# A streaming encoder trunk in fp32r: the last channel tile's gate and store issued earlier, the second half's layer norm written between matmul products, eight tiles for the feed-forward squares

## The chip, the cores and the metric

The kernel runs on one core of one Trainium2 chip. The time is the device time of one launch in microseconds, the median of three runs: 1488.08 us (1486.97 to 1489.66). The engines are TensorE (PE, matrix products), VectorE (DVE), ScalarE (ACT), GpSimd (POOL) and SyncE (SP), which issues most of the loads and stores. Each engine works through its own instructions in the order in which they stand in its program, and waits on semaphores for the others.

## The reference

A trunk of two layers for 512 prompt frames and 8 x 16 sample frames, 640 columns in all, with 1024 channels:

```python
def conv_module(h, hist, g, w_pw1, b_pw1, w_dw, b_dw, ln_g, ln_b, w_pw2, b_pw2):
    a, gate = jnp.split(rms_norm(h, g) @ w_pw1 + b_pw1, 2, axis=-1)
    glu = a * jax.nn.sigmoid(gate)
    full = jnp.concatenate([hist.astype(glu.dtype), glu], axis=1)
    y = lax.conv_general_dilated(full, w_dw[:, None, :], window_strides=(1,), padding="VALID", ...) + b_dw
    y = jax.nn.silu(layer_norm(y, ln_g, ln_b))          # depthwise, width 31; mean and variance per frame
    return h + y @ w_pw2 + b_pw2, full[:, -CONV_HIST:]

def swiglu_ffn(h, g, w_in, w_out):
    a, b = jnp.split(rms_norm(h, g) @ w_in, 2, axis=-1)
    return h + (jax.nn.silu(a) * b) @ w_out

# layer 0: h = conv_module(h); h = swiglu_ffn(h)
# layer 1: h = h + attention(rms_norm(h), shared k, v) @ w_o; h = swiglu_ffn(h); at the end rms_norm(h)
```

The outputs are the normed frames, the keys and values, and the last 30 columns of `glu` of every stream.

## The kernel before

Channels lie on the partitions: `h` has eight channel tiles of 128 partitions by 640 columns. The columns are worked in two halves of 320 (index `g`, 0 or 1; half 0 holds the 128 sample columns and 192 prompt columns, half 1 the other prompt columns). A float32 product is made of three fp32r products: a weight tile `raw` is split into `whi` (rounded, by ACT) and `wlo` (the rest, by DVE), an operand into `xh` and `xl` the same way, and `mm3` (L179 to L185) adds hi x hi, lo x hi and hi x lo. `wsplit` (L133) loads a weight tile and splits it; there are two buffers of each kind. The feed-forwards combine quarter blocks in the manner of Strassen, seven products in place of eight; `X11`, `X21`, `XT4`, `X22` are operands of them, and `XH` and `XL` are their two parts.

**The convolution.** For every channel tile c, `glu_` (L713) makes the two products of the pointwise layer, the tanh (ACT, L726) and the gate (DVE, L733 for the sample columns, L739 for the prompt columns), which writes `gall`. Tiles 0 to 2 are convolved tap by tap on DVE (`conv_taps`, L764 to L779) and POOL. Tiles 3 to 7 are convolved on PE: `conv_shift` (L805) stores the gated tile to a buffer in device memory (`sa` for half 0, `sb` for half 1), `conv_read` (L811) reads it back four times, each shifted by one column (`xa`, `xb`), and `conv_pe` (L818, matmuls at L832) multiplies the copies. The string `PLAN` sets the order in which this is written: `E7` is the gate of tile 7's half 0 with its store and reads, `F7` that of half 1, `S7 A7` its convolution for half 0, `e` the taps of tile 2 on DVE, `n` the layer norm of half 0, `m` that of half 1, `w0 w1` the second pointwise layer of each half.

**The layer norm.** `conv_ln` (L838) goes in four steps, separated by `yield`: the mean (sums on DVE, L212, then matmuls with a column of 1/1024, L221), its spread over the partitions (matmuls with the identity, L233), the subtraction, squares on ACT and their sums (L867); the variance's mean; its spread; the scaling, silu and split into the operands `z`. `staged_ln` (L896) writes the steps of half 0 between the convolutions of tiles 5, 6 and 7 for half 1. `pw2` (L906) makes the second pointwise layer: four weight tiles, each for two channel tiles of the output, 48 matmuls of 320 columns each, 192 for a half; DVE adds the result to `h` (L924).

**The feed-forward's norm.** `stats` (L556) squares the eight tiles of `h`, adds them up, and spreads the reciprocal root over the partitions; the squares pass through two buffers in turn. `xnorm` multiplies it into the operands. `std` (L430) makes the plain products. `MEAN_AT`, `SPREAD_AT` and `STATS1_AT` are the places among earlier products at which the matmuls of the norms stand.

**What sets the order.** The program is written in the order of the source and then put in order engine by engine by a scheduler that goes by its own estimate of the times. The source steers it: `tc.high_priority` lets work go ahead, `tc.issue_after(x)` and `behind(...)` keep work behind an instruction x that is written earlier. On SP and in the engines' queues nothing overtakes afterwards.

Of the kernel before, what the change touches and what calls it, by code (L numbers as in the profile page):

```python
# [15 lines left out]
P = 128  # L16
D = 1024
# [19 lines left out]
MEAN_AT, SPREAD_AT, STATS1_AT = 3, 5, 2  # L37
# [7 lines left out]
GAPS = 1, 12, 2  # L45
# [36 lines left out]
def tile_trunk(ctx, tc, xT, vecs, hist, w_pw1, w_pw2, w_in0, w_out0, w_os0, w_in1, w_out1, w_os1,  # L82
# [50 lines left out]
    def wsplit(src, k, n, parts=1, pool=0, cuts=1, gains=None):  # L133
# [18 lines left out]
        with tc.high_priority(offset=HP):  # L152
            for i in range(cuts):
                a, b = sz * i // cuts, sz * (i + 1) // cuts
                nc.scalar.activation(out=hi[:, a:b], in_=raw[:, a:b], func=AF.Copy)
                c = b - (b - a) * pool // 4
                for eng, a, b in ((nc.vector, a, c), (nc.gpsimd, c, b)):
                    if a < b:
                        eng.tensor_tensor(out=lo[:, a:b], in0=raw[:, a:b],  # L159
                                          in1=hi[:, a:b].bitcast(F32), op=ALU.subtract)  # L160
        return hi, lo
# [68 lines left out]

    def spread(st, r, n, ins=False):
        for t, a in enumerate(tiles(n)):
            end = nc.tensor.matmul(st[:, a:a + P], r[:, t:t + 1].to_broadcast([P, P]), ident,  # L233
                                   start=True, stop=True)
        return end.ins if ins else st[:, :n]
# [68 lines left out]
    def ffn(l, w_in, w_out, w_os, tail, hf, lead=(), b0=None):  # L304
# [280 lines left out]
        with tc.high_priority(offset=HP):  # L585
# [4 lines left out]
            with tc.issue_after(put_end[0]):  # L590
                xnorm(x21, 0, 4)
# [114 lines left out]
    glu_end, gate_end, conv_end, sum_end = [None], [None], [None], [None]  # L706
# [57 lines left out]
    def conv_taps(chains, limit):  # L764
        for i in range(W):
            for c, part, dst, js in chains:
# [10 lines left out]
                else:  # L777
                    nc.vector.scalar_tensor_tensor(out=dst, in0=src, scalar=wj, in1=dst,
                                                   op0=ALU.mult, op1=ALU.add)  # L779
# [25 lines left out]
    def conv_shift(c, tag, c0, n, late=False):  # L805
        nt = NXA if tag == "a" else NXB
        sc = dr.tile([P, nt], F32, tag="s" + tag, name=nm("s" + tag), bufs=3)[:, 0:n]
        nc.sync.dma_start(sc, gall[:, c, c0:c0 + n])
        return (lambda: conv_read(sc, tag, n, nt)) if late else conv_read(sc, tag, n, nt)

    def conv_read(sc, tag, n, nt):  # L811
        x4 = cp.tile([P, 4, nt], F32, tag="x" + tag, name=nm("x" + tag), bufs=2)
        for s in range(4):
            nc.sync.dma_start(x4[32 * s:32 * s + 32, :, 0:n - s],
                              sc[:, s:n].rearrange("(q p) w -> p q w", q=4))
# [90 lines left out]
    def pw2(g, z):  # L906
        n = gr[g][1]
        for m2 in M2[g]:
            if (KT, m2) not in pws:
                pws[KT, m2] = wsplit(w_pw2[m2], 16, P, pool=PL2[g])  # L910
# [5 lines left out]
            for ks in [range(k, k + 1) for k in range(KT)] if both else [range(KT)]:  # L916
                for i in range(2):
                    mm3(pair[i], [(wh[:, (i * 8 + k) * P:(i * 8 + k + 1) * P],
                                   wl[:, (i * 8 + k) * P:(i * 8 + k + 1) * P]) for k in ks],
                        xk(z, ks), ks[0] == 0, ks[-1] == KT - 1)  # L920
# [8 lines left out]
    def step(op, arg):  # L929
# [17 lines left out]
        elif op in "CDEF":  # L947
            if op != "F":
# [8 lines left out]
                nc.sync.dma_start(convs_out[:, c], gs[:, c])  # L957
            if op != "E":
                glu(c, 1, *pws[c])
                if op != "D":  # L960
                    x4s[c][2] = conv_shift(c, "b", NSC + HA, NXB, c == KT - 1)
# [553 lines left out]
```

## Time and profile before

| | us |
|---|---|
| median of three runs | 1488.08 |
| profiled run | 1485.55 |
| its span | 1483.6 |
| PE busy | 1429.4 (96%) |
| DVE busy | 1138.3 (77%) |
| ACT busy | 757.2 (51%) |
| POOL busy | 297.7 (20%) |
| DMA | 192.56 MB, 130 GB/s on average |

The profile shows one execution. Its times count from the span's start. A row of a timeline gives the start, the time that the group of equal instructions took, the engine, the line, the operation, output<-inputs, the number of instructions and, in square brackets, how long the engine had been idle before it and what ended that. `SPq` is SP's queue of DMA issues: the time there is that of the issue, not of the transfer. Matmuls overlap, so the distance of their starts, not the duration of one, is the pace.

### The profile page before, as it was taken

Reading aid. Unit: us, or ns where it says so; the run is one execution under the profiler, and the core shown is the slowest. Engines: PE = TensorE matmul, PEld = TensorE weight load, DVE = VectorE, ACT = ScalarE, POOL = GpSimd, SP = SyncE. Lnnn points to the kernel's source line nnn. Section 1 sums busy time; section 2 is a strip of 40 time slices with the busy share of each in tenths; the row PEclk is TensorE's granted clock in tenths of the full one; section 3 lists DMA queues with packets and bytes.
Section 4 is the critical chain, followed back from the end, with each engine's and each line's share of the span. In section 5 each row is a group of like instructions: output and inputs, shape, how many; then the busy total and the mean of one; then the engine's idle time right before and its main releaser. Section 6 shows DMA issues by size and latency. Waiting matters only on the chain.

```text
span 1483.6 us, 28030 instructions
## 1 busy us (share of the span) xinstructions
PE 1429.4 (96%) x10932; PEld 1365.9 (92%) x10932; DVE 1138.3 (77%) x2523; ACT 757.2 (51%) x1620; POOL 297.7 (20%) x356
## 2 busy tenths in 40 slices
PE   5999899999999999999999999999999999999997
PEld 5998699999999999999988888987899999999997
DVE  5789656799888888866766767566799888888755
ACT  3666245465454564445655454443565455455443
POOL 5789102001111111103222112010001111111101
PEclk9999999999999999999999999999999999999999
DMA  7256514125445444433655555361224444544512
GB/s 239 68 160 189 138 58 136 36 75 143 131 116 133 134 118 130 132 109 133 212 164 204 180 173 193 129 208 23 86 75 129 138 118 117 150 118 108 153 64 72
DMA packets 66660, 192.56 MB, mean 130 GB/s; under 512 B 12000, under 2 KB 30176, under 8 KB 58080
## 3 DMA queue, kind: packets, MB, share of 16 engines
q1 hardware_dynamic: 52736, 161.10, 33.5%
q0 software_dynamic: 13504, 29.37, 9.7%
q8 instruction: 86, 1.41, 0.4%
q14 instruction: 46, 0.38, 0.1%
q10 hardware_dynamic: 288, 0.31, 0.1%
HBM read 179.14 MB, written 11.61 MB: 129 GB/s over the span
## 4 chain that ended last, share of the span: by engine, by line
PE 77%; DVE 8%; POOL 6%; ACT 3%; DMA 3%; issue 3%; SPq 0%; POOLq 0%; DVEq 0%; ACTq 0%
PE mm L409 46%; PE mm L182 8%; PE mm L183 7%; PE mm L184 7%; POOL ca L788 5%; PE am L1226 1%; PE am L1209 1%; PE w L221 1%; PE w L1242 1%; ACT whi L147 1%; PE am L1273 1%; DVE wlo L343 1%; PE mm L832 1%; DVE B L446 1%; PE w L1185 1%
## 5 line engine op out<-in xcount | busy, mean ns | idle before, releaser
L409 PE MATMUL mm<-XH,wlo 128*128 128x320 f32 x896 | 276.9, 310 | 0.0
L409 PE MATMUL mm<-XH,whi 128*128 128x320 f32 x896 | 276.1, 311 | 0.7 <-ACT t L419 0.5
L409 PE MATMUL mm<-XL,whi 128*128 128x320 f32 x896 | 274.4, 310 | 0.0
L342 ACT ACTIVATE whi<-raw 128x512 fp32r<-128x512 f32 (+2 forms) x280 | 169.2, 614 | 141.3 <-PE mm L409 116.5
L182 PE MATMUL mm<-xh,whi 128*128 128x320 f32 (+2 forms) x640 | 202.5, 318 | 6.4 <-ACT xh L171 4.2
L343 DVE TENSOR_TENSOR wlo<-raw,whi 128x512 fp32r<-128x512 f32 (+2 forms) x280 | 184.9, 668 | 22.4 <-ACT whi L342 21.0
L183 PE MATMUL mm<-xh,wlo 128*128 128x320 f32 (+2 forms) x640 | 201.1, 315 | 0.6 <-DVE wlo L159 0.6
L184 PE MATMUL mm<-xl,whi 128*128 128x320 f32 (+2 forms) x640 | 198.4, 313 | 0.0
L409 PE MATMUL mm<-hid,whi 128*128 128x320 f32 x732 | 171.4, 310 | 2.2 <-DVE hid L343 2.2
L409 PEld LDWEIGHTS mm<-XH,whi 128*128 128x128 f32 x896 | 168.4, 189 | 2.1 <-ACT t L419 1.3
L409 PEld LDWEIGHTS mm<-XH,wlo 128*128 128x128 f32 x896 | 169.0, 189 | 0.0
L409 PEld LDWEIGHTS mm<-XL,whi 128*128 128x128 f32 x896 | 167.9, 188 | 0.0
L182 PEld LDWEIGHTS mm<-xh,whi 128*128 128x128 f32 x640 | 122.5, 192 | 9.7 <-ACT xh L171 5.0
L409 PEld LDWEIGHTS mm<-hid,whi 128*128 128x128 f32 x732 | 124.8, 188 | 4.2 <-DVE hid L343 3.2
L183 PEld LDWEIGHTS mm<-xh,wlo 128*128 128x128 f32 x640 | 122.9, 192 | 1.0 <-DVE wlo L159 0.8
L184 PEld LDWEIGHTS mm<-xl,whi 128*128 128x128 f32 x640 | 121.8, 191 | 0.4 <-issue 0.2
L409 PE MATMUL mm<-hid,wlo 128*128 128x320 f32 x366 | 112.9, 308 | 0.0
L409 PE MATMUL mm<-XL,shi 128*128 128x320 f32 x344 | 105.5, 308 | 5.0 <-DVE XL L343 5.0
L409 PE MATMUL mm<-XH,shi 128*128 128x320 f32 x344 | 105.8, 308 | 0.7 <-ACT XH L342 0.7
L409 PE MATMUL mm<-XH,slo 128*128 128x320 f32 x344 | 105.7, 307 | 0.0
L388 POOL DMA_DIRECT2D s<-in_w_in x38 | 22.1, 581 | 386.2 <-DVE wlo L343 207.9
L788 POOL TENSOR_TENSOR ca<-ca,cvt 128x512 f32<-128x512 f32 x60 | 91.7, 1528 | 15.0 <-ACT cvt L785 8.0
(255 smaller groups left out, 3345.2 us busy)
## 6 DMA issues: line engine op xcount, KB each, us to landing
raw<-in_w_in SPq DMA_DIRECT2D x38, 1024.0 KB
s<-in_w_in POOLq DMA_DIRECT2D x76, 256.0 KB, 4.2
raw<-in_w_os SPq DMA_DIRECT2D x24, 768.0 KB
cache<-in_ck SPq DMA_DIRECT2D x32, 512.0 KB
cache<-in_cv SPq DMA_DIRECT2D x32, 512.0 KB
raw<-in_w_pw SPq DMA_DIRECT2D x12, 1024.0 KB
s<-in_w_os POOLq DMA_DIRECT2D x48, 192.0 KB, 3.6
raw<-in_w_kq SPq DMA_DIRECT2D x8, 1024.0 KB
```

The source lines that it names most:

```text
L147: nc.scalar.activation(out=hi[:, a:b], in_=raw[:, a:b], func=AF.Copy, scale=gain)
L182: nc.tensor.matmul(ps, wh, xh, start=(first and i == 0), stop=False)
L183: nc.tensor.matmul(ps, wl, xh, start=False, stop=False)
L184: end = nc.tensor.matmul(ps, wh, xl, start=False, stop=(stop and i == last))
L221: mean_end[0] = nc.tensor.matmul(st[:, 512 + t * w + k:513 + t * w + k], s[:, a:a + P], onec, start=True, stop=True).ins
L342: put_end[1] = nc.scalar.activation(out=hi, in_=src, func=AF.Copy).ins
L343: put_end[0] = nc.vector.tensor_tensor(out=lo, in0=src, in1=hi.bitcast(F32), op=sub).ins
L388: nc.gpsimd.dma_start(s1, src[:, 2 * n:3 * n])
L409: last = nc.tensor.matmul(pt, wt, v, start=(first and k == i == 0), stop=(k == n - 1 and i == 2), skip_group_check=True)
L446: nc.vector.scalar_tensor_tensor(out=out, in0=x, scalar=-1.0, in1=y, op0=mult, op1=op)
L788: nc.gpsimd.tensor_tensor(out=acc, in0=acc, in1=pr, op=ALU.add)
L832: conv_end[0] = nc.tensor.matmul(pt[32 * q:32 * q + 32, 0:n], w4[0:r, 4 * tg + q, :], mv, start=(tg == 0), stop=(tg == 7)).ins
```

## The change

Two stretches of the program get another order, the end of the convolution up to the head of the first feed-forward and the end of the attention up to the head of the second. The number of instructions on each engine stays the same.

1. The first half of tile 7: its store and reads are written ahead of tile 6's half-1 reads and of the output store; the weight loads `w_pw2[0]` and `w_pw2[1]` are issued around tile 6, that of `w_pw2[0]` without its split, and the loads of `w_pw2[2]` and `[3]` stand behind tile 7's half-1 reads.
2. On DVE the taps of tile 2 are parted: 24 behind tile 7's first gate, 13 behind its second gate (token `f`), where the split of `w_pw2[0]` stands too. In the sums of the first mean tiles 2 and 3 change places.
3. The second half's layer norm is written between the products of `pw2(0)`, in gaps of 5, 3, 10 and 4 pieces of six matmuls (`GAPS1`), and the rest behind it. Counted in matmuls of `pw2` on PE: the mean stands behind 30 where it stood behind none (its last third behind 21), its spread behind 48 (43), the variance's mean 60 behind that spread (118), the variance's spread 24 behind its mean (27), and 60 matmuls of this half follow it (4).
4. The feed-forward's norms are placed by 4, 6, 1 (`MEAN_AT`, `SPREAD_AT`, `STATS1_AT`) instead of 3, 5, 2. In the first feed-forward the second half's mean stands behind 74 products (86), its spread 40 behind that (45), and 30 products lie between the spread and the first product with `XT4` (13). In the second they are 97 (98), 23 (40) and 24 (6); there a tie in `std` keeps the second pair of products of the third weight behind the spread.
5. `stats` has a tile of its own for each of the eight squares.

On SP, before, from the store of tile 6's half 1 (`sb`) to the store of tile 7's half 0 (`sa`); `raw` is a weight load, `xb` the shifted reads of tile 6, `out_convs` an output store:

```order
L808 DMA sb_1566<-gall 128x350
L144 DMA raw_2403<-in_w_pw 128x2048
L814 DMA xb_1568<-sb_1566 32x4x350
L814 DMA xb_1568<-sb_1566 32x4x349
L814 DMA xb_1568<-sb_1566 32x4x348
L814 DMA xb_1568<-sb_1566 32x4x347
L957 DMA out_convs<-gall 128x368
L808 DMA sa_1672<-gall 128x590
```

And now, from the same store on; `xa` are the shifted reads of tile 7:

```order
L815 DMA sb_1571<-gall 128x350
L815 DMA sa_1666<-gall 128x590
L983 DMA out_convs<-gall 128x368
L821 DMA xa_1668<-sa_1666 32x4x590
L821 DMA xa_1668<-sa_1666 32x4x589
L821 DMA xa_1668<-sa_1666 32x4x588
L821 DMA xa_1668<-sa_1666 32x4x587
L821 DMA xb_1673<-sb_1571 32x4x350
```

The store moved past a weight load, four reads and an output store, and tile 7's reads past those of tile 6.

On DVE, before, around the gate of tile 7's half 1 (L739); `w_174` is the chain of taps of tile 2, `w_113` another such chain, `acc` the sums of the first mean:

```order
L778 SCALAR_TENSOR_TENSOR w_113_789<-gall,dwv,w_113_789 128x128
L778 SCALAR_TENSOR_TENSOR w_174_1225<-gall,dwv,w_174_1225 128x128 x13
L739 SCALAR_TENSOR_TENSOR gall<-t_226_1836,t_227_1838 128x320
L159 TENSOR_TENSOR wlo_2347<-raw_2345,whi_2346 128x2048
L212 TENSOR_TENSOR acc_1986<-y_102 128x320
L212 TENSOR_TENSOR acc_1986<-acc_1986,y_102 128x320 x5
```

And now, at the same place:

```order
L785 SCALAR_TENSOR_TENSOR w_174_1225<-gall,dwv,w_174_1225 128x128 x5
L746 SCALAR_TENSOR_TENSOR gall<-t_229_1827,t_230_1829 128x320
L785 SCALAR_TENSOR_TENSOR w_174_1225<-gall,dwv,w_174_1225 128x128 x4
L160 TENSOR_TENSOR wlo_1434<-raw_1432,whi_1433 128x2048
L785 SCALAR_TENSOR_TENSOR w_174_1225<-gall,dwv,w_174_1225 128x128 x9
L215 TENSOR_TENSOR acc_1992<-y_102 128x320
L215 TENSOR_TENSOR acc_1992<-acc_1992,y_102 128x320 x5
```

Thirteen taps moved from ahead of this gate to behind it, in two groups around the split. Ahead of tile 7's first gate, the gate of tile 6's half 1 moved in and five taps moved out; the split of 2048 columns stands ahead of it in both.

On DVE in the second half's norm, before, from the subtraction of the mean on (`acc` are the sums of the squares `sql`, `h` the additions of the products):

```order
L851 TENSOR_TENSOR y_103<-y_103,w_255_2191 128x320 x8
L924 SCALAR_TENSOR_TENSOR h<-mm_2293,vec,h 128x320
L924 SCALAR_TENSOR_TENSOR h<-mm_2294,vec,h 128x320
L159 TENSOR_TENSOR wlo_2405<-raw_2403,whi_2404 128x2048
L867 TENSOR_TENSOR acc_2227<-sql_2223 128x320
L924 SCALAR_TENSOR_TENSOR h<-mm_2351,vec,h 128x320
L867 TENSOR_TENSOR acc_2227<-acc_2227,sql_2223 128x320
```

And now:

```order
L943 SCALAR_TENSOR_TENSOR h<-mm_2197,vec,h 128x320
L943 SCALAR_TENSOR_TENSOR h<-mm_2198,vec,h 128x320
L858 TENSOR_TENSOR y_103<-y_103,w_260_2229 128x320 x8
L160 TENSOR_TENSOR wlo_2353<-raw_2351,whi_2352 128x2048
L874 TENSOR_TENSOR acc_2283<-sql_2279 128x320
L943 SCALAR_TENSOR_TENSOR h<-mm_2299,vec,h 128x320
L874 TENSOR_TENSOR acc_2283<-acc_2283,sql_2279 128x320
```

The two additions to `h` moved ahead of the subtractions; both splits of weights still stand ahead of the last sums.

The diff, cut to what bears on this:

```diff
-MEAN_AT, SPREAD_AT, STATS1_AT = 3, 5, 2
+MEAN_AT, SPREAD_AT, STATS1_AT = 4, 6, 1
-GAPS = 1, 12, 2
+GAPS, GAPS1 = (1, 12, 2), (5, 3, 10, 4)
-LNO = ((0, 1, 4, 5, 6, 2, 3, 7), (0, 1, 4, 2, 3, 5, 6, 7))
-PLAN = ("a0 y x1 b0 b1 q0 dp1s0 c2 k ds1p2 D3 C4 S3 q3 ds2 C5 E6 S4 A4 F6 B4 E7 e S5 A5 F7 k k k S6 A6 "
-        "S7 A7 n s0 m w0 w1")
-HELD = {(1, 0): 21, (2, 0): 9}
+LNO = ((0, 1, 4, 5, 6, 3, 2, 7), (0, 1, 4, 2, 3, 5, 6, 7))
+PLAN = ("a0 y x1 b0 b1 q0 dp1s0 c2 k ds1p2 D3 C4 S3 q3 ds2 C5 E6 S4 A4 F6 B4 E7 e S5 A5 F7 f k k k S6 A6 "
+        "S7 A7 n s0 m w1")
+HELD, HELD2 = {(1, 0): 21, (2, 0): 4}, {(2, 0): 14}
...
-        def std(ws, half, sink):
+        def std(ws, half, sink, second=None):
             pa, pb = mmt()[:, :NH], mmt()[:, :NH]
             for k, x in enumerate(((X11, X21), (XT4, X22))[half]):
-                xproduct(pa, ws[k], x, k == 0)
-                ends.append(xproduct(pb, ws[2 + k], x, k == 0).ins)
+                with tc.issue_after(second) if k and second else nullcontext():
+                    xproduct(pa, ws[k], x, k == 0)
+                    ends.append(xproduct(pb, ws[2 + k], x, k == 0).ins)
...
-                            (nc.gpsimd, nc.vector)[half], half == 1)
+                            (nc.gpsimd, nc.vector)[half], half == 1, sqs=x12 + x22)
...
-            with tc.issue_after(put_end[0]):
+            with nullcontext() if b0 is None else tc.issue_after(put_end[0]):
                 xnorm(x21, 0, 4)
...
-            std(wstd[jj], 0, sinks[jj])
+            std(wstd[jj], 0, sinks[jj], jj == 2 and b0 is not None and norm_spread[0])
...
-            with tc.issue_after(conv_end[0]):
+            with behind(conv_end[0], tap_end[0]):
                 next(ln, None)
...
-                pws[KT, m2] = wsplit(w_pw2[m2], 16, P, pool=PL2[g])
+                with tc.issue_after(read_end[0]):
+                    pws[KT, m2] = wsplit(w_pw2[m2], 16, P, pool=PL2[g])
...
+            if both:
+                for k in range(KT):
+                    part(0, range(k, k + 1))
+                    part(1, range(k, k + 1))
+                    yield
+            else:
                 for i in range(2):
...
+                    for k in range(0, KT, 2):
+                        part(i, range(k, k + 2))
+                        yield
...
-                else:
-                    pws[KT, 0] = wsplit(w_pw2[0], 16, P)
                 glu_(c, 0, *pws[c], None)
-                x4s[c] = [w4, conv_shift(c, "a", 0, NSC if op == "D" else NXA), None]
-                nc.sync.dma_start(convs_out[:, c], gs[:, c])
+                read = conv_shift(c, "a", 0, NSC if op == "D" else NXA, True)
+                if c + 2 == KT:
+                    pws[KT, 0] = wsplit(w_pw2[0], 16, P, late=True)
+                    with tc.issue_after(store_end[0]):
+                        pws[KT, 1] = wsplit(w_pw2[1], 16, P)
+                x4s[c] = [w4, read(), None]
+                if c + 1 == KT:
+                    with tc.issue_after(read_end[0]):
+                        x4s[c - 1][2] = x4s[c - 1][2]()
+                with tc.issue_after(store_end[0]):
+                    nc.sync.dma_start(convs_out[:, c], gs[:, c])
...
         elif op == "e":
             with tc.issue_after(gate_end[0]):
-                conv_taps(held, {})
+                conv_taps(held, HELD2)
...
+        elif op == "f":
+            with behind(gate_end[0], glu_end[0]):
+                conv_taps(held, {})
+                pws[KT, 0] = pws[KT, 0]()
...
         elif op == "m":
-            for _ in conv_ln(1, sum_end[0]):
+            ln, products = conv_ln(1, sum_end[0]), pw2(0, zs[0])
+            for gap in GAPS1:
+                for _ in range(gap):
+                    with tc.issue_after(conv_end[0]):
+                        next(products)
+                with tc.issue_after(conv_end[0]):
+                    next(ln, None)
+            while next(products, 0) is None:
                 pass
         elif op == "w":
-            pw2(c, zs[c])
+            for _ in pw2(c, zs[c]):
+                pass
```

More of the change, by code (lines that the diff above doesn't have):

```diff
@@ L151, in wsplit, with split @@
             return hi, lo
[L152 to L161, printed above, removed]
+        def split():
+            with tc.high_priority(offset=HP):
+                for i in range(cuts):
+                    a, b = sz * i // cuts, sz * (i + 1) // cuts
+                    nc.scalar.activation(out=hi[:, a:b], in_=raw[:, a:b], func=AF.Copy)
+                    c = b - (b - a) * pool // 4
+                    for eng, a, b in ((nc.vector, a, c), (nc.gpsimd, c, b)):
+                        if a < b:
+                            eng.tensor_tensor(out=lo[:, a:b], in0=raw[:, a:b],
+                                              in1=hi[:, a:b].bitcast(F32), op=ALU.subtract)
+            return hi, lo
+        return split if late else split()
     @contextmanager
@@ L234, in spread @@
                                    start=True, stop=True)
+        norm_spread[0] = end.ins
         return end.ins if ins else st[:, :n]
@@ L704, in w4t @@
         return cp.tile([P, 1024], F32, tag="w4", name=nm("w4"), bufs=3)
-    glu_end, gate_end, conv_end, sum_end = [None], [None], [None], [None]
+    glu_end, gate_end, conv_end, sum_end, store_end, read_end, tap_end = ([None] for _ in range(7))
     def glu(c, g, wh, wl, mid=None):
```

24 lines of the change are left out of this document (13 added, 11 removed).

## The prediction

> **What bounds the kernel.** The page's table of busy time comes first:
>
> ```profile
> PE 1429.4 (96%) x10932; PEld 1365.9 (92%) x10932; DVE 1138.3 (77%) x2523; ACT 757.2 (51%) x1620; POOL 297.7 (20%) x356
> ```
>
> TensorE (PE) is busy for 96% of the span of 1483.6 us, so only PE's idle time, 54.2 us in all, and stretches at a low clock can be won back by a change of order. The next view is PE's waits between 130 and 300 us, where the conv module ends and the first feed-forward begins; a row gives the total, the count and the longest wait:
>
> ```profile
> PE mm L832 <- DMA xa<-sa: 6.1, 1, 6.1
> PE mm L409 <- DVE XL L343: 2.9, 2, 2.2
> ```
>
> The largest, 6.1 us, is a single wait for a DMA, the shifted copies of the last channel tile. The third view is the chain of waits, read forward to that wait (start, length, what):
>
> ```profile
> 147.46 3.96 DVE w L778 x16
> 151.42 4.56 DMA sa<-gall
> ...
> 159.09 6.50 DMA xa<-sa
> ...
> 165.72 6.77 PE mm L832 x128
> ```
>
> From the start of the store to the arrival of the copies is 159.09 + 6.50 − 151.42 = 14.2 us. The fourth view, busy times by stretch, gives the granted clock (PEclk, the column after POOL) around the waits:
>
> ```profile
> 164.00:170.00 6.00, 4.28 (x76) 4.08 (x80) 0.00 (x0) 0.37 (x1) 0.00 (x0) 0.50 0.72 174
> ...
> 194.00:198.00 4.00, 4.00 (x21) 4.00 (x19) 1.79 (x4) 2.29 (x6) 0.00 (x0) 0.57 0.00 0
> ...
> 226.00:228.00 2.00, 0.92 (x6) 0.88 (x6) 2.00 (x6) 2.00 (x5) 0.00 (x0) 1.00 0.00 0
> 228.00:232.00 4.00, 3.48 (x15) 3.26 (x14) 2.78 (x7) 4.00 (x10) 0.00 (x0) 0.57 0.00 0
> ...
> 290.00:293.00 3.00, 3.00 (x13) 3.00 (x13) 3.00 (x8) 0.48 (x2) 0.00 (x0) 0.50 0.00 0
> ```
>
> After a wait PE runs for a while at half clock. A stretch of 4 us at 0.57 loses 4 × 0.43 = 1.7 us; I use that as the price of one such stretch.
>
> **The last tile's first half.** The timelines of PE, ScalarE (ACT), VectorE (DVE) and SyncE (SP) show why the store starts so late:
>
> ```profile
> 153.75 0.31 PE L183 MATMUL mm<-xh,wlo 128*128 128x320 f32 x1
> ...
> 154.78 0.31 PE L184 MATMUL mm<-xl,whi 128*128 128x320 f32 x1
> 155.02 4.57 PE L832 MATMUL mm<-xa,w 128*32 128x128 f32 x128
> 165.72 6.77 PE L832 MATMUL mm<-xa,w 128*32 128x128 f32 x128 [6.13 <-DMA xa<-sa]
> 172.43 0.83 PE L221 MATMUL w<-onec,acc 128*128 128x1 f32 x6
> ```
>
> ```profile
> 144.12 0.52 ACT L726 ACTIVATE t<-mm,hb 128x320 f32<-128x320 f32 x1
> 155.19 0.53 ACT L726 ACTIVATE t<-mm,hb 128x320 f32<-128x320 f32 x1 [3.05 <-PE mm L184]
> ```
>
> ```profile
> 142.26 2.28 DVE L159 TENSOR_TENSOR wlo<-raw,whi 128x2048 fp32r<-128x2048 f32 x1
> 144.46 1.92 DVE L778 SCALAR_TENSOR_TENSOR w<-gall,dwv,w 128x128 f32<-128x128 f32 x5
> 146.29 0.91 DVE L733 SCALAR_TENSOR_TENSOR gall<-t,t 128x128 f32<-128x128 f32 x1
> 147.12 0.35 DVE L739 SCALAR_TENSOR_TENSOR gall<-t,t 128x192 f32<-128x192 f32 x1
> 147.38 9.96 DVE L778 SCALAR_TENSOR_TENSOR w<-gall,dwv,w 128x128 f32<-128x128 f32 x32
> 157.25 0.49 DVE L739 SCALAR_TENSOR_TENSOR gall<-t,t 128x320 f32<-128x320 f32 x1
> 157.65 2.29 DVE L159 TENSOR_TENSOR wlo<-raw,whi 128x2048 fp32r<-128x2048 f32 x1
> 159.85 0.48 DVE L212 TENSOR_TENSOR acc<-y 128x320 f32<-128x320 f32 x1
> 160.37 2.67 DVE L212 TENSOR_TENSOR acc<-acc,y 128x320 f32<-128x320 f32 x5
> ```
>
> ```profile
> 148.29 1.74 SPq L814 DMA_DIRECT2D xb<-sb  x4
> 150.14 1.19 SPq L957 DMA_DIRECT2D out_convs<-gall  x1
> ```
>
> The gate was ready at 147.47; the store stood on SP behind four reads and an output store until 151.42. In the new order nothing but the earlier tile's store stands ahead of it there. On DVE five taps (1.92) leave the place ahead of the gate, and a 0.49 gate of the sixth tile's second half comes in: with the split ending at 144.5 and the tanh at 144.64, the gate is ready near 146.1 and the store follows at once. With the 14.2 us of before as the upper bound (a load of weights and the reads of xb, which shared the DMA engines then, are elsewhere now) the copies arrive by 160.3. PE needs them at 159.59, the end of the row at 155.02. So the wait of 6.13 falls to between 0 and 0.7, and the 128 matmuls take 4.57 again, not 6.77: PE is through at 164.2 to 164.9, where it was at 172.4.
>
> What is late next is DVE. Thirteen taps of tile 2 now stand behind the gate of the last tile's second half, whose tanh ends at 155.72. One chain of dependent taps costs 1.92/5 = 0.38 each, so: gate 0.41, taps 13 × 0.37 = 4.8, split 2.2, six sums 3.1, end near 166.2. (The other 24 taps cost 24 × 9.96/32 = 7.5 and end by 153.6, before that tanh: hidden.) The mean at 172.43 therefore begins near 166.2, after a PE wait of 1.3 to 2.0. **Gain 6.2.** Whether such a wait brings a half-clock stretch is open, 0 or 1.7; I take off the middle, 0.8. The moved reads of xb feed matmuls that stand behind that mean, and the output store has no reader: both cost nothing unless the reads, now behind those of xa, land after it.
>
> **The second half's layer norm.** These rows price it:
>
> ```profile
> 202.34 3.27 DVE L851 TENSOR_TENSOR y<-y,w 128x320 f32<-128x320 f32 x8 [3.62 <-PE w L233]
> ...
> 215.14 1.01 DVE L867 TENSOR_TENSOR acc<-acc,sql 128x320 f32<-128x320 f32 x2
> ```
>
> ```profile
> 227.08 0.41 PE L182 MATMUL mm<-xh,whi 128*128 128x320 f32 x1 [1.58 <-ACT xh L171]
> 228.74 0.64 PE L182 MATMUL mm<-xh,whi 128*128 128x320 f32 x1 [0.52 <-DVE h L924]
> ```
>
> Before, four products followed the last spread, and PE then waited 1.58 + 0.52 for the normed tiles, with the half-clock stretch at 228 behind it: 3.8 us. Now the rest of the 192 products of the first half, 60 of them, stand behind that spread; at a pace of (154.78 − 153.75)/7 = 0.147 they cover 8.8 us, so these 3.8 go. But the variance's mean now follows the first spread after 60 products (8.8 us), where it had 118. In DVE's order stand between that spread and the last sum: eight subtractions (3.2), two splits (2 × 2.2 to 2.3), and four additions to h and seven sums, of the same 320 columns, at 0.41 (3.27/8) to 0.50 (1.01/2) each, 4.5 to 5.5. That is 12.1 to 13.3, less the two additions that can start while the spread still runs (up to 0.8). PE waits 2.5 to 4.5; I take 3.3, nearer the lower end because the operations overlap at their ends in the trace, and a half-clock stretch behind it, 1.7, as after the 2.1 us at 227. The block of means that precedes the stretch at 194 keeps its size, so that stretch stays. **Net loss 5.0 − 3.8 = 1.2**; ends 1.3 gained (wait 2.5, no stretch) and 2.4 lost (wait 4.5).
>
> **The feed-forward heads.** The rows with waits and the spreads ahead of them:
>
> ```profile
> 282.37 0.83 PE L233 MATMUL w<-ident,rst 128*128 128x128 f32 x6
> 288.76 0.41 PE L409 MATMUL mm<-XL,shi 128*128 128x320 f32 x1 [2.19 <-DVE XL L343]
> ...
> 1066.43 0.83 PE L233 MATMUL w<-ident,rst 128*128 128x128 f32 x6
> 1068.88 0.41 PE L409 MATMUL mm<-XH,shi 128*128 128x320 f32 x1 [0.73 <-ACT XH L342]
> 1073.22 0.41 PE L409 MATMUL mm<-XL,shi 128*128 128x320 f32 x1 [2.04 <-DVE XL L343]
> ```
>
> In the first feed-forward the second half's operand was ready 5.56 us after the spread (283.20 to 288.76), of which PE worked 3.37. Seventeen more products now stand in that gap: 3.37 + 17 × 0.147 = 5.87, enough by 0.3. The wait of 2.19 and the stretch at 290 (1.7) go: **gain 3.9**, ends 2.5 and 3.9. In the second feed-forward eighteen more stand there, 2.6 us against waits of 0.73 + 2.04 = 2.77: **gain 2.3**, between 0, if the waits only move on, and 2.6; I give 0.3 back, since DVE works without a pause there. The sums of squares must be ready twelve products, 1.8 us, sooner; eight tiles in place of two let ACT square without waiting for the adder to release one. These squares lie beside 74 products (10.9 us) and cost PE nothing; if that cover failed, each of them would add one operation of 320 columns, 0.5 at most.
>
> **Sum.** 6.2 − 0.8 − 1.2 + 3.9 + 2.3 = 10.4 us. The profiled run took 1485.55 us, 2.5 less than the median of 1488.08; 1485.55 − 10.4 = 1475.1 there, and 1477.7 as a median.
>
> By the Trainium skill ("TensorE: Matmul & The Clock Gate", Part 1, the clock gate) the array drops to half rate after at least one idle window of about 3.4 us. The stretches here agree with that length, but waits of 2.1 and 2.19 us were enough to bring one, so in this kernel partly idle windows count, and I charge the stretch.
>
> **The rivals.** (a) Part of the tile-7 gain comes back: the store meets other traffic or the sums on DVE end later, and the clock drops at both new waits. Half of 6.2, another 0.9 for the clock: about 1481.7; 16%. For it: DVE has no idle time between 155.7 and 166 in my schedule.
> (b) DVE is the bound in both feed-forward heads and the earlier spread only moves the waits: 6.2 returns, 1483.9; 12%. For it: the margin of 0.3; against it: the waits end on operands whose whole chain starts at the spread.
> (c) The clock does not drop at the new waits of 2.0 and 3.3: 2.5 less, 1475.2; 12%. This is also what the rule of the Trainium skill's page on the clock gate would give.
> (d) Slower. The loads of the last two pointwise weights now stand on SP behind this row:
>
> ```profile
> 179.43 1.74 SPq L814 DMA_DIRECT2D xb<-sb  x4
> ```
>
> With the 6 us gained they go out near 175; a tile of 128 x 2048 numbers of four bytes, 1.05 MB, at 174 GB/s (the rate of the stretch at 164) takes 6 us, so both land by 187. The spread ended by 202.34; 6.2 earlier and with 5 more products ahead of it that is 196.8, DVE comes to the two splits near 201 and 207, and the sums end near 209. So the loads are hidden by 14 to 20 us. If the second load got its buffer only from the first one's split (203), it would land at 209; with its two halves of the split (about 2 and 2.3) and the last sums the end is near 214.5, which is 5.4 later and another stretch of 1.7: 1484.8, no longer surely faster. From a landing at about 215 it decides for slower: 11.7 later and 1.7 is 1491.1. 5%; against it, the weights that were in both buffers before are split by 160 in my schedule.
>
> The forecast itself, 1474.5 to 1480.5, has 50%; 5% are left for (a) or (b) together with a mild (d), within the bound of measurement, which is 0.2% or 3 us. Of (b) a fourth lies within it too. So faster is 50 + 16 + 9 + 12 = 0.87, same 5 + 3 = 0.08, slower 0.05. The range 1472 to 1484 takes in (a), (c) and most of (b).
>
> **What would show it.** In the new profile: no PE wait on xa, or one under 1; the store of the last tile near 146; the first mean near 166 with a wait on DVE's sums of 1 to 2; a new PE wait of about 3.3 at the variance's mean, and none for normed tiles behind the last spread; no wait on XL in the two heads; half clock gone at 290, present near the variance's mean. The forecast is wrong if the split ahead of the gate waits for its load (each microsecond then delays the store), if the 13 taps run longer, or if a load is late.

## The result, and the profile after

The changed kernel takes 1478.53 us (median of 4 runs, 1477.44 to 1480.16) against 1488.87 for the kernel before (4 runs, 1486.97 to 1489.8): a ratio of 0.9933, 95% interval 0.9916 to 0.9950. The forecast was 1477.7, in a range of 1472 to 1484. The profiled run took 1477.44 with a span of 1474.9, 8.7 less than the span of 1483.6 before.

PE's busy time went from 1429.4 to 1425.7, the rest of the gain is idle time. These are PE's waits of the changed kernel between 130 and 300 us, in the view that showed xa and XL before:

```profile
PE w L224 <- DVE acc L874: 4.3, 2, 3.6
PE mm L839 <- issue: 1.3, 1, 1.3
PE w L224 <- DVE acc L215: 0.9, 1, 0.9
PE w L238 <- POOL rst L881: 0.2, 1, 0.2
```

The wait of 6.1 for xa is gone, and so are those for XL and for the normed tiles. New are 3.6 at the variance's mean of the second half (L874), as the prediction had it, 0.9 at the first mean (L215), and 1.3 "issue", for nothing that the profile shows, inside the last tile's matmuls. The clock by stretches (PEclk is the column after POOL):

```profile
160.00:164.00 4.00, 2.73 (x89) 2.28 (x81) 3.68 (x12) 0.85 (x3) 0.00 (x0) 1.00 0.48 88
164.00:168.00 4.00, 3.10 (x54) 2.46 (x45) 2.38 (x5) 0.42 (x1) 0.00 (x0) 1.00 0.02 4
190.00:194.00 4.00, 4.00 (x34) 4.00 (x34) 1.53 (x5) 0.58 (x2) 0.00 (x0) 1.00 0.00 0
...
208.00:216.00 8.00, 7.80 (x34) 7.80 (x35) 0.85 (x3) 0.00 (x0) 0.85 (x1) 0.57 0.40 131
```

Only one half-clock stretch is left ahead of the end of the kernel, behind the wait of 3.6, and it is twice as long as any one wait had drawn at the pointwise products before: the clock's own record has it from 208.4 for 6.83 us. Four were there before. This is one profiled execution: five of the kernels below, with the same order of matmuls there, show a further stretch between 192 and 200 us.

The same landmarks on PE in both traces tell where the time was won. The first mean began at 172.43 and begins at 166.71. The feed-forwards' first products, and a wait that both have in the middle of the first and of the second feed-forward, before:

```profile
260.15 0.31 PE L409 MATMUL mm<-XH,shi 128*128 128x320 f32 x1
...
354.69 0.41 PE L409 MATMUL mm<-hid,shi 128*128 128x320 f32 x1 [0.58 <-ACT hid L342]
...
1016.96 0.33 PE L1260 MATMUL am<-ident,Ss 128*128 128x128 f32 x1 [0.74 <-ACT PTs L1262]
...
1137.43 0.41 PE L409 MATMUL mm<-hid,shi 128*128 128x320 f32 x1 [0.54 <-DVE hid L343]
```

and after:

```profile
166.71 0.83 PE L224 MATMUL w<-onec,acc 128*128 128x1 f32 x6 [0.91 <-DVE acc L215]
...
255.91 0.31 PE L415 MATMUL mm<-XH,shi 128*128 128x320 f32 x1
...
345.69 0.41 PE L415 MATMUL mm<-hid,shi 128*128 128x320 f32 x1 [0.58 <-ACT hid L348]
...
1008.80 0.33 PE L1298 MATMUL am<-ident,Ss 128*128 128x128 f32 x1 [0.73 <-ACT PTs L1300]
...
1128.58 0.41 PE L415 MATMUL mm<-hid,shi 128*128 128x320 f32 x1 [0.55 <-DVE hid L349]
```

| stage | lead at its end | of this stage | forecast |
|---|---|---|---|
| to the first mean | 5.7 | +5.7 | +5.4 (6.2 less 0.8 for the clock) |
| to the first feed-forward's begin | 4.2 | −1.5 | −1.2 |
| to its middle | 9.0 | +4.8 | +3.9 |
| to the end of the attention | 8.2 | −0.8 | 0 |
| through the second feed-forward's head | 8.9 | +0.7 | +2.3 |
| end of the span | 8.7 | −0.2 | 0 |

### The profile page after: what moved, and what is told of

Read it like the earlier page. It is cut to its first block, busy times and chain, and to the rows that moved or that the text cites. A ratio compares the mean times of both kernels' runs of the same rounds, so it can differ in the third digit from the quotient of the medians.

```text
span 1474.9 us, 28018 instructions
## 1 busy us (share of the span) xinstructions
PE 1425.7 (97%) x10932; PEld 1363.0 (92%) x10932; DVE 1139.2 (77%) x2523; ACT 755.3 (51%) x1620; POOL 297.6 (20%) x356
## 4 chain that ended last, share of the span: by engine, by line
PE 80%; DVE 8%; POOL 5%; ACT 3%; issue 2%; DMA 2%; POOLq 0%; DVEq 0%; ACTq 0%
PE mm L415 46%; PE mm L185 8%; PE mm L187 8%; PE mm L186 8%; POOL ca L795 4%; PE am L1264 1%; DVE wlo L349 1%; PE w L1280 1%; PE w L224 1%; PE am L1247 1%; PE mm L839 1%; ACT whi L147 1%; PE am L1311 1%; PE w L1223 1%; DMA raw<-in_w_os 1%
```

## The experiments

The medians below stand beside runs of the kernel before on the same chip; the ratio and its interval are against those.

**The place on SP.** Tile 6's reads and the output store go ahead of the last tile's store again, DVE's order stays:

```diff
+                if c + 1 == KT:
+                    x4s[c - 1][2] = x4s[c - 1][2]()
+                    outs = nc.sync.dma_start(convs_out[:, c], gs[:, c]).ins
+                    with behind(read_end[0], outs):
+                        read = conv_shift(c, "a", 0, NXA, True)
...
                 x4s[c] = [w4, read(), None]
-                if c + 1 == KT:
-                    with tc.issue_after(read_end[0]):
-                        x4s[c - 1][2] = x4s[c - 1][2]()
```

> The changed kernel with one thing put back: on SP, tile 6's half-1 reads and the output store of tile 7 stand ahead of tile 7's first store again; DVE's order stays as changed. Theory A (the place on SP is the cause of the old 6.1 us wait, since the gate ends at 147.45 in the changed kernel as it ended at 147.47 before): the store goes out near 151 again, the copies arrive 11 to 14 us later, PE waits 3 to 6 us for xa, the first mean begins at 168 to 171 instead of 166.7, and the time is 2 to 5 us above the changed kernel's 1478.5. Theory B (the gain comes from what stands on DVE): the first mean stays within 0.5 us of 166.7 and the time within 1 us.

Measured: 1486.48, 0.9989 (0.9975 to 1.0002), nearly all of the gain gone. In the changed kernel SP's timeline was:

```profile
147.46 0.34 SPq L815 DMA_DIRECT2D sa<-gall  x1
147.84 0.82 SPq L983 DMA_DIRECT2D out_convs<-gall  x1
150.31 1.74 SPq L821 DMA_DIRECT2D xa<-sa  x4
```

SP's timeline and PE's, of this run:

```profile
149.28 1.73 SPq L821 DMA_DIRECT2D xb<-sb  x4
151.10 0.38 SPq L975 DMA_DIRECT2D out_convs<-gall  x1
151.57 0.38 SPq L815 DMA_DIRECT2D sa<-gall  x1
...
166.20 7.30 PE L839 MATMUL mm<-xa,w 128*32 128x128 f32 x128 [7.37 <-DMA xa<-sa]
```

The store goes out at 151.57, as before, and PE waits 7.4. The first mean begins at 173.43. Theory A holds, and by more than I had given it: SP had no weight load ahead of this store or beside it, and its copies still arrived only near 166, 14.6 after the store. The clock adds to it (half clock from 161.6 for 10.2 us). The order on SP alone makes the first stage's gain.

**More products ahead of the variance's mean.**

```diff
-GAPS, GAPS1 = (1, 12, 2), (5, 3, 10, 4)
+GAPS, GAPS1 = (1, 12, 2), (5, 3, 16, 4)
```

> The changed kernel with 16 pieces (96 products, 14.1 us) instead of 10 (60) between the second half's first spread and the variance's mean. Theory A (the wait of 3.6 us on DVE's sums and the two half-clock windows behind it, 3.4 us, come from too few products there): the wait is under 0.3, no half-clock stretch near 208, the first feed-forward begins 6 to 7 us earlier, at 249 to 250, the time is near 1472. Theory B (DVE is the bound here, and what is saved at the variance's mean is waited for behind the last spread, where now 21 products stand for 60): a wait of 2 to 4 us for the normed tiles, the feed-forward begins less than 3.5 us earlier, the time is 1475 or more.

Measured: 1475.08, 0.9923 (0.9896 to 0.9950). The median is 3.5 below the changed kernel's and the span 3.1, but the intervals of the two ratios overlap, so the gain rests on the trace. PE's waits:

```profile
PE mm L839 <- issue: 2.1, 1, 2.1
PE mm L415 <- DVE XL L349: 1.4, 2, 0.8
PE w L224 <- DVE acc L874: 0.7, 1, 0.7
```

The wait of 3.6 and its half-clock stretch are gone, and the feed-forward begins at 249.44, 6.5 earlier: theory A on the cause. But waits on XL of 0.8 and 0.6 come up in the first feed-forward's head, and its middle is reached only 4.7 earlier (341.02): of 6.5, 1.8 is given back there, which is theory B in part. In the changed kernel PE's wait had given DVE the time to be ready for the head, so that the old wait of 0.74 at its begin went too; that 0.7 of the table's +4.8 belongs to the −1.5.

**The layer norm written as before.**

```diff
-            ln, products = conv_ln(1, sum_end[0]), pw2(0, zs[0])
-            for gap in GAPS1:
...
+            for _ in conv_ln(1, sum_end[0]):
+                pass
...
-        "S7 A7 n s0 m w1")
+        "S7 A7 n s0 m w0 w1")
```

> The changed kernel with the second half's layer norm written as before, without gaps (the variance's mean 118 products behind the spread, 4 products behind the last one). Theory A (this part of the change costs, as I counted, 1.2 us): the wait of 3.6 and the two half-clock windows at 208 go, waits of 1.6 + 0.5 for the normed tiles and a half-clock stretch near 222 return, perhaps the one near 188 too; the feed-forward begins 1 to 3 us earlier than the changed kernel's 255.9, the time is 1476 to 1478. Theory B (the interleaving is worth something by itself): the feed-forward begins later than 255.9 and the time is above 1479.

Measured: 1479.29, 0.9950 (0.9932 to 0.9968), not to be told from the changed kernel. PE's waits:

```profile
PE mm L839 <- issue: 2.2, 1, 2.2
PE mm L185 <- ACT xh L174: 1.6, 1, 1.6
PE mm L415 <- DVE XL L349: 1.4, 2, 0.8
...
PE mm L185 <- DVE h L943: 0.5, 1, 0.5
```

The waits of 1.6 and 0.5 are back, the 3.6 is gone, no half-clock stretch follows, and the feed-forward begins at 253.57, 2.3 earlier, as theory A had it. The stop in the last tile's matmuls ("issue") is longer in this run and draws a half-clock stretch, so the first mean is 1.4 later (168.13); counted from that mean, the plain order is 3.8 shorter (85.4 against 89.2). It is given back as in the run with 16 pieces: waits of 0.8 and 0.6 on XL, and the second feed-forward begins only 0.4 earlier. So the interleaving as it was set won nothing here; with 16 pieces it does.

**The places of the feed-forward norms.**

```diff
-MEAN_AT, SPREAD_AT, STATS1_AT = 4, 6, 1
+MEAN_AT, SPREAD_AT, STATS1_AT = 3, 5, 2
```

> The changed kernel with the feed-forward norms at the old places (3, 5, 2). Theory A (the places alone made the gain in the two heads): in the first feed-forward a wait of about 2.2 on XL with a half-clock stretch returns and the time from the feed-forward's begin to its middle grows by 3 to 4.8 us; in the second about 2 us on XL return; in all the time is 3 to 5.5 us above 1478.5. Theory B (the eight tiles and the earlier arrival of the data did it): under 1 us in each head, the time within 1.5 us of 1478.5.

Measured: 1479.37, 0.9943 (0.9924 to 0.9962). Theory A falls: the first feed-forward's head has no wait, as in the changed kernel, and the second has these:

```profile
PE w L1402 <- DVE sqs L1395: 1.0, 1, 1.0
PE mm L415 <- DVE XL L349: 0.6, 1, 0.6
```

The changed kernel has 1.55 for the squares, 0.37 for `h` and 0.57 for XL there; the last of these stands in its timeline as

```profile
1063.08 0.41 PE L415 MATMUL mm<-XL,shi 128*128 128x320 f32 x1 [0.57 <-DVE XL L349]
```

The numbers gain nothing; in the second head they cost 0.9 of wait, and in four of the ten kernels profiled with the new numbers the wait of 1.55 also drew a half-clock stretch (1.7 us), in none of the three with the old ones. PE's order shows why nothing is gained: with the old numbers the second half's mean and spread stand behind the same 74 and 40 products in the first feed-forward, and 97 and 23 in the second, as with the new ones. What made the gain had to be something else that the change does in the heads, and the next three runs part it.

**The squares in two buffers.**

```diff
-                            (nc.gpsimd, nc.vector)[half], half == 1, sqs=x12 + x22)
+                            (nc.gpsimd, nc.vector)[half], half == 1)
```

> The changed kernel with the feed-forward squares in two buffers again, all places as changed. Theory A (the eight tiles are off PE's path, as I costed them): the two heads keep their waits of 0 (first) and 1.55 + 0.57 (second) within 0.3 us, the squares on ACT wait again for the adders, the time is within 1.5 us of 1478.5. Theory B (the eight tiles made the gain in the heads, since with the places put back the waits did not return): waits of 1 to 2.2 us on XL come back in one or both heads, and the time is 1.5 to 5 us longer.

Measured: 1480.39, 0.9956 (0.9938 to 0.9974). The waits in both heads are those of the changed kernel within 0.03 us, and ACT waits for POOL's adder 5.9 us in all without PE noticing. Theory A: the eight tiles are off the path. The median is 1.9 higher with overlapping intervals; the one larger wait that the changed kernel lacks (1.38 on `h`) lies at 589 us, far from the squares. The run with the old places, which has the eight tiles, waits 0.88 there, so the two buffers are not needed for it; what brings it is not settled.

**The tie on the first feed-forward's operand.**

```diff
-            with nullcontext() if b0 is None else tc.issue_after(put_end[0]):
+            with tc.issue_after(put_end[0]):
                 xnorm(x21, 0, 4)
```

> The changed kernel with the tie put back that keeps the second operand of the first feed-forward behind the first one's split. In PE's order this alone puts the second half's mean behind 87 products instead of 74 and its spread 45 behind that instead of 40. Theory A (the distance from that spread to the products that read XL decides): the wait of about 2.2 at XL and the half-clock stretch behind it return, 3 to 4 us in the first feed-forward, time 1481 to 1483. Theory B (the eight tiles decide): no wait on XL over 0.6 in the first feed-forward, time within 1 us of 1478.5.

Measured: 1481.26, 0.9958 (0.9943 to 0.9972). The wait returns, 2.20 against 2.19:

```profile
PE w L224 <- DVE acc L874: 3.6, 1, 3.6
PE mm L415 <- DVE XL L349: 2.2, 1, 2.2
```

Theory A: this one line, which moves the mean from 87 to 74 products and leaves 30 of them behind the spread, made the first head's gain. The half-clock stretch did not come with the wait this time, so the cost up to the middle of the feed-forward was 2.5 and not 3.9.

**The tie in the second feed-forward.**

```diff
-            std(wstd[jj], 0, sinks[jj], jj == 2 and b0 is not None and norm_spread[0])
+            std(wstd[jj], 0, sinks[jj], None)
```

> The changed kernel without the tie in the plain products of the second feed-forward (the second pair of products of the third weight behind the spread). Theory A (the products kept behind the spread cover DVE's way to XL there): waits of 1 to 2.7 us on XH and XL return in the second feed-forward, where 0.57 was left, and the begin-to-middle time of that stage grows by 0.7 to 2.2 us. Theory B (the eight tiles or the places did it): the waits stay at 0.6 within 0.3.

Measured: 1481.66, 0.9969 (0.9951 to 0.9987). PE's waits in the second head:

```profile
PE w L1402 <- DVE sqs L1395: 1.6, 1, 1.6
PE mm L415 <- DVE XL L349: 1.1, 1, 1.1
PE mm L415 <- DVE hid L450: 0.9, 1, 0.9
PE mm L415 <- ACT XH L348: 0.6, 1, 0.6
PE mm L415 <- DVE h L1343: 0.4, 1, 0.4
```

Waits of 1.1 + 0.9 + 0.6 = 2.6 stand where 0.57 was, and the stage up to the middle of that feed-forward is 2.6 longer, somewhat more than theory A's 2.2, since a wait of 0.9 at 1119 comes with it. Theory A: this tie is the second head's gain.

**What sets the gate.** In the changed kernel the gate was ready at 147.45, not at 146.1. DVE's timeline of the changed kernel:

```profile
144.29 1.58 DVE L746 SCALAR_TENSOR_TENSOR gall<-t,t 128x320 f32<-128x320 f32 x1
145.80 1.37 DVE L740 SCALAR_TENSOR_TENSOR gall<-t,t 128x128 f32<-128x128 f32 x1
147.09 0.35 DVE L746 SCALAR_TENSOR_TENSOR gall<-t,t 128x192 f32<-128x192 f32 x1
```

The test leaves one operand of the first two gates in PSUM:

```diff
-            a = tp.tile([P, tw[0]], F32, tag="t2", name=nm("t2"))
+            a = ps[0] if (c, g) in ((6, 1), (7, 0)) else tp.tile([P, tw[0]], F32, tag="t2", name=nm("t2"))
```

> The changed kernel with one operand of two gates (tile 6's half 1, tile 7's half 0) left in PSUM instead of SBUF; same numbers, same order. In the changed kernel these gates took 1.58 and 1.37 us, each ending about when an addition of POOL ended, where the same shapes took 0.49 and 0.30 elsewhere. Theory A (a DVE operation with both tensors in SBUF waits for POOL's running addition): the gates take under 0.6 and 0.5, the store goes out 1.5 to 2 us earlier, near 145.7; the time stays within 1 us, since PE then waits for DVE's sums. Theory B (the gates wait for something else, ACT's results or the strided write): their durations stay over 1 us and the store stays near 147.4.

Measured: 1484.88, 0.9981 (0.9968 to 0.9994). DVE's timeline:

```profile
143.60 0.48 DVE L746 SCALAR_TENSOR_TENSOR gall<-t,mm 128x320 f32<-128x320 f32 x1
147.67 0.29 DVE L740 SCALAR_TENSOR_TENSOR gall<-t,mm 128x128 f32<-128x128 f32 x1 [3.59 <-ACT t L733]
147.87 0.35 DVE L746 SCALAR_TENSOR_TENSOR gall<-t,mm 128x192 f32<-128x192 f32 x1
```

On the durations theory A holds: 0.48 and 0.29 in place of 1.58 and 1.37, the first inside one of POOL's additions (141.51 to 144.82), the second beside another POOL operation (147.50 to 149.41). On the store it does not, and the time is 6 us longer: PSUM is now held until the gate, which stands behind the split on DVE, so PE waits 2.4 for the tanh of the gate before (a wait that no other run has), half clock follows from 141.9 for 3.4 us, and everything behind it is later. The cure cost more than the trouble.

**The stop inside the last tile's matmuls.** PE stops for 1.3 us ahead of 162.8 in the changed kernel, and 1.5 to 2.2 in the six other runs above that have the early reads and leave the gates in SBUF:

```profile
155.24 6.30 PE L839 MATMUL mm<-xa,w 128*32 128x128 f32 x190
162.82 2.98 PE L839 MATMUL mm<-xa,w 96*32 96x128 f32 x66 [1.27 <-issue]
```

The trace's DMA records show one transfer of 16 KB on the instruction queue at 160.1 to 161.4 (161.0 to 162.2 in the run with 16 pieces), and PE goes on 1.2 to 1.5 us after its end; in the kernel before, that transfer came 2.0 us behind the begin of tile 6's matmuls, now 4.8. That it brings PE's instructions is inferred: in every run with the stop, PE stops at the same matmul, the 191st of the 256, whatever the time. Two runs ask what holds the transfer up. The first moves an output store of 1024 small packets:

```diff
         x4s[7][2] = x4s[7][2]()
+        with tc.issue_after(read_end[0]):
+            nc.sync.dma_start(convp_out, gp[:, :, T:T + HIST])
```

> The changed kernel with one output store, of 1024 rows of 120 bytes, issued 18 us later, behind the reads of tile 7's half 1. In the changed kernel PE stops for 1.3 us (2.1 in two of the runs) inside the last tile's 128 matmuls, for nothing that the profile shows; a 16 KB transfer of the instruction queue ended 1.3 us before it went on, 2.8 us later in the stage than in the kernel before. Theory A (the small packets hold up the fetch of PE's instructions): the stop is gone or under 0.4, the matmuls end near 164.2, and the first mean still waits for DVE until 166.7. Theory B (PE runs through 256 such matmuls faster than its instructions come, whatever else moves): the stop stays between 1 and 2.2. The time is within 1 us of 1478.5 either way.

Measured: 1480.43, 0.9955 (0.9941 to 0.9970). The stop is 1.65: theory A falls, the small packets are not it. (The store's new place made reads of tile 7's half 1 late, a wait of 1.3 at 182.) The second moves the reads of tile 6 instead:

```diff
-                if c + 1 == KT:
-                    with tc.issue_after(read_end[0]):
-                        x4s[c - 1][2] = x4s[c - 1][2]()
...
                     x4s[c][2] = conv_shift(c, "b", NSC + HA, NXB, c >= KT - 2)
+                if c + 1 == KT:
+                    with tc.issue_after(store_end[0]):
+                        x4s[c - 1][2] = x4s[c - 1][2]()
```

> The changed kernel with tile 6's half-1 reads issued behind the store of tile 7's half 1, near 157 instead of 152. Theory A (the fetch of PE's instructions, which ended at 161.5, waits behind the packets of these reads): the 16 KB transfer comes 2 us or more earlier, the stop of 1.3 to 2.1 us inside the last tile's matmuls is gone or under 0.5, and they end near 164.2. Theory B (PE asks for the block when it gets there, and the fetch takes its time whatever else moves): the stop stays. The first mean stays near 166.7 in both, since DVE's sums end then.

Measured: 1481.87, 0.9969 (0.9958 to 0.9981). The stop is gone; the matmuls of tiles 6 and 7 run through. The DMA view of the stretch from 156 to 160 us, in the changed kernel:

```profile
q1 hardware_dynamic: 625, 0.84, 106.8%
```

and in this run:

```profile
q1 hardware_dynamic: 548, 0.75, 82.3%
q8 instruction: 1, 0.02, 2.0%
```

With the reads out of the way the 16 KB come at 157.3, inside this stretch. Theory A: the place of the reads decides when the transfer comes, and with it the stop. That it stood behind their packets is the reading that fits: in the changed kernel it starts at 160.1, and the last of these packets ends at 160.7. But the time did not fall. PE's timeline:

```profile
154.88 8.93 PE L839 MATMUL mm<-xa,w 128*32 128x128 f32 x256
166.35 1.44 PE L224 MATMUL w<-onec,acc 128*128 128x1 f32 x6 [2.54 <-DVE acc L215]
```

DVE's sums end when they did, so the 1.3 + 0.9 become one wait of 2.5, and this one brings half clock from 166.3 for 6.8 us, which the two short ones had not.

**A version from what was learned.** The third gap has 16 pieces, the norms' places are 3, 5, 2, the reads go later as above, and two edits shorten DVE's way to the first mean:

```diff
-HELD, HELD2 = {(1, 0): 21, (2, 0): 4}, {(2, 0): 14}
+HELD, HELD2 = {(1, 0): 21, (2, 0): 4}, {(2, 0): 18}
...
                 conv_taps(held, {})
-                pws[KT, 0] = pws[KT, 0]()
...
                 next(ln, None)
+            if callable(pws[KT, 0]):
+                with tc.issue_after(add_end[0]):
+                    pws[KT, 0] = pws[KT, 0]()
```

(`add_end` is the last addition of the mean's sums.)

> A version made from the runs so far: 16 pieces in the third gap, the norm places 3, 5, 2, the split of the first pointwise weight behind the first mean's sums, four more taps ahead of the last gate, and the reads of tile 6's half 1 behind the store of tile 7's half 1. If each does what the runs showed or what the rows give: first mean at 163.5 to 164.5 instead of 166.7 (2 to 3 us), no wait and no half clock at the variance's mean (4 us net, as in the run with 16 pieces), 0.9 in the second feed-forward: 1470 to 1473. If DVE or the loads are the bound behind it, waits on XL at the first feed-forward's head grow by what is gained, and the time is 1474 to 1476.

Measured: 1470.60, 0.9897 (0.9880 to 0.9913), faster than both kernels, 7.9 below the changed one. The first mean begins at 164.28, no half-clock stretch is left ahead of the kernel's end, and these are PE's waits between 130 and 300 us:

```profile
PE mm L415 <- DVE XL L349: 1.4, 2, 0.9
PE w L224 <- DVE acc L874: 0.7, 1, 0.7
PE mm L186 <- DVE wlo L160: 0.5, 1, 0.5
PE w L238 <- POOL rst L881: 0.2, 1, 0.2
```

## Why the prediction was right, point by point

**The last tile's first half: right in place and nearly in size, wrong in one step.** Forecast 6.2 for the mean, measured 5.7. The step that failed is "the gate is ready near 146.1": it was ready at 147.45, as before, because tile 6's gate ahead of it took 1.58 instead of 0.49, and its own first operation 1.37 instead of 0.91. I had priced them by rows and had not asked what else ran. The Trainium skill ("SBUF — State Buffer", section "SBUF: two separate sides") states that of a DVE operation with two SBUF inputs and a GpSimd operation that reads SBUF, the one that starts first holds the shared port pair for its whole length and the other is blocked; the trace and the run with one operand in PSUM agree (0.48 and 0.29 there). It cost nothing, since "the copies arrive by 160.3" had used 14.2 us from store to arrival; in the trace's DMA records the copies are through at 157.4, 10 us after the store. So the whole gain is the place on SP, which one run shows. "End near 166.2" for DVE's sums was 166.7. The possible half-clock stretch, charged at half, did not come: the stop's 1.27 and the mean's 0.91 fell into two windows of the clock (last section).

**The second half's layer norm: right in the wait, lucky in the clock.** Forecast a wait of 3.3 and a net loss of 1.2; measured 3.6 and 1.5. Two errors of the clock cancel: the stretch behind the wait was two windows, 6.8 us, which is 3.4 lost and not 1.7; and the one at 194, of which I had written "that stretch stays", is missing in this profile. Its absence is luck: five other kernels with the same order of matmuls there have it, between 192 and 200 us (`heads_back` from 192.3, `sp_order` from 199.2, each for 3.41). With it the loss would have been about 3.2. In this profile the block of means lay across a border of the clock's windows (last section). The rival by which the clock would not drop here is out.

**The first feed-forward's head: right, for the reason given (products between the spread and XL).** 3.9 forecast, 4.8 measured. The excess is the wait of 0.74 at its begin, which went because DVE gained time while PE waited at 208. Which edit brings the products there I had not said; it is the removed tie and not the three numbers.

**The second head: the mechanism was right, the term mis-sized.** The 2.77 us of waits fell to 0.57, as forecast, by the tie in `std`. But 2.3 net became 0.7: the new numbers (MEAN_AT and the other two, put back together in one run) raised the wait for the squares from 0.98 to 1.55 and brought 0.37 for `h`, and 0.58 more came up further on at 1127, with the old numbers too. I had put the shift of the means at nothing.

**What was taken as free.** The eight tiles: right, no wait of PE depends on them. The loads behind tile 7's reads (rival d): they went out at 175.6, as reckoned at 175, and nothing waited for them. Some 0.8 us were given back between the two heads, where I had 0: the wait near 460 us grew by 0.5 and one of 0.2 at 455 is new.

The sum, 10.4, is to be held against 8.7 in the span and 8.1 in the profiled runs; the medians lie 10.3 apart. The median's near hit is in part luck: the runs of either kernel lie up to 3 us apart.

## What to carry to other kernels

Look on the queue, not only at the data: a store whose data is ready still waits for every issue that stands ahead of it, and in this kernel the order of a few DMA issues was worth more than the rest of the change (put back, it left a ratio of 0.9989 where the whole change has 0.9933). When norm steps are put between matmul products, count the products against the other engine's whole way between two steps: 60 products against 12 us of DVE made a wait of 3.6, 96 made none. A gain at one stage feeds the next one's wait; take the landmarks of two traces side by side before calling it won.

## What the runs showed of the hardware that was not expected

- The same wait does not always bring the same loss of clock; where it lies decides. The wait of 3.6 at the variance's mean stood in nine of the kernels profiled and drew 6.83 us of half clock in six, 3.41 in three. In each trace the half-clock stretches begin whole multiples of 3.41 us apart (in the kernel before at 163.48, 194.20, 228.34 and 289.78: 9, 19 and 37 windows behind the first), so each trace shows its own grid of windows. The Trainium skill ("TensorE: Matmul & The Clock Gate", Part 1) states that such windows run freely; the traces agree. Count PE's idle time inside single windows, from 60 to 1455 us of all thirteen traces: each of the 17 windows with 2.07 us or more was followed by half clock, and six of the 17 with 1.46 to 1.79. The wait of 3.6 put 3.15 to 3.38 us into one window in the six kernels, 2.50 to 3.02 in the three. The wait of 2.19 for XL lay in one window and drew a stretch; the 2.20 in the run with the tie lay across a border, 1.50 and 0.71, and drew none. Matmuls of one column act like idle time: the second half's mean is a block of 18 or 24 of them, 2.2 to 2.7 us without a pause, and half clock followed it in all six kernels in which 2.17 us or more of it lay in one window, in none of the seven in which at most 1.93 did. One case stays open: 2.53 of idle time in the run with later reads drew 6.83.
- PE can run out of instructions, as far as the runs tell. 256 small matmuls in 9 us, with their weight loads, outran a 16 KB transfer of the instruction queue that came only as the packets of four shifted reads ended; the stop was 1.3 to 2.2 us and vanished when the reads went out 4 us later.
- A DVE gate of 320 columns took 1.58 us instead of 0.49 while POOL added tiles, and 0.48 inside such an addition once an operand lay in PSUM.
